# Turning activation tiles with VectorE blocks and ScalarE copies in place of TensorE transposes

## The chip, the cores and the metric

The kernel runs on one core of one Trainium2 chip. The metric is device time in microseconds, from the first to the last instruction of one execution, as the median over runs. TensorE (PE) does matrix products into PSUM, its weight loads (PEld) run beside them; VectorE (DVE) and ScalarE (ACT) work elementwise; GpSimd (POOL) does almost nothing here; SyncE (SP) issues the DMAs.

## The reference

One decoder layer, 256 tokens of 2048 channels, all float32: a SwiGLU FFN (5632 wide), a mixer with two branches, a second FFN. Each is normalised, modulated by a conditioning vector c through w_ada, and added to x. Cut to what matters:

```python
mod = (silu(c) @ w_ada + b_ada).reshape(B, 9, 1, D)

h = modulate(rms_norm(x, g_ffn1), mod[:, 0], mod[:, 1])
x = x + 0.5 * mod[:, 2] * swiglu(h, w_ffn1_gu, w_ffn1_down)    # (silu(g) * u) @ w_down

h = modulate(rms_norm(x, g_mix), mod[:, 3], mod[:, 4])
u_pool, q, k, v, ga, gb = split(h @ w_in)
y_pool = multiscale_pool(u_pool, pool_mix, pool_scale) @ w_pool_up
y_attn = swa_sink_attention(q, k, v, ...) @ w_attn_up
merged = sigmoid(ga) * y_pool + sigmoid(gb) * y_attn
x = x + mod[:, 5] * (merged @ w_o)

h = modulate(rms_norm(x, g_ffn2), mod[:, 6], mod[:, 7])
x = x + 0.5 * mod[:, 8] * swiglu(h, w_ffn2_gu, w_ffn2_down)
```

## The kernel before

**Sets.** Every large product is a `Set`: up to 1024 output columns, for both tiles of 128 tokens, over all rows of the weight. The stationary operand is a block of 128 channels by 128 tokens, so activations are kept with channels on the partitions; the weight rows move. Four PSUM banks hold a set's sums (two token tiles by two chunks of 512 columns); the other four banks, `bank()`, serve small work and then the next set. A ktile is 128 rows of a weight. `run` (line 205) goes over the ktiles: each load brings 1 MB, two ktiles at 1024 columns or four at 512, into a `raw` tile, of which there are six (`RAW`).

**Split products.** Each float32 product is three: hi*hi, lo*hi, hi*lo. `prep` (line 172) makes the halves of a weight ktile: ScalarE copies it rounded (`wh`, line 180), VectorE subtracts (`wl`, line 184). There are three buffers of each. `mm` (line 187) issues the products, lines 194, 196 and 198. Activations that come from a turned tile are split by `split_stat` just ahead of their product (lines 297 and 298: `sh` and `sl`, or `hh` and `hl`).

**Order.** The program says what is done in a dictionary of hooks after which ktile. A scheduler then draws up each engine's order at compile time: of what is ready, the instruction that stands first in the program goes first, so that an engine can do later work while it would wait. A tile's buffer is taken from the free ones when its first instruction can go.

**FFN.** `ffn` (line 400) takes the 5632 activation columns in pieces of 1024, the last of 512. For each piece a set makes the gate products, `silu_to` (line 386) brings them to SBUF as `sg`, another set makes the up products, and `times` (line 391) multiplies, on VectorE (line 395). The result has tokens on the partitions; the down product needs channels there. `store_T` (line 378) returns the pieces of that turn, and the next set runs them after its ktile 3. For each two blocks of 128 channels, `pair_T` (line 221) has TensorE transpose four 128x128 blocks into one PSUM bank (line 225), and ScalarE copies the bank to the tile `actT` (line 382; its name in the profile is `big`). The first FFN's first three pieces are finished together during the first norm, their parts waiting inside `actT` and in `sg`, and all three are turned in the set after them. After the last piece come two down sets of 44 ktiles.

**Mixer.** The merged rows come in two halves of 1024 columns. Each is finished by lines 736 and 737 on VectorE, and turned into `mT` (line 742) in the same way as above, by `tr` at ktile 3 of the next set: the next gate set for the first half, the output projection w_o for the second. The projection uses the second half from its ktile 8 on.

**Side work.** Sums over w_ada for later stages run beside the products: `ada_item` loads 1 MB into a `raw` tile and adds it up on VectorE (line 129). 0.82 such items go with each weight load in the first FFN, 0.56 in the mixer, 0.15 in the second FFN.

Of the kernel before, what the change touches and what calls it, by code (L numbers as in the profile page):

```python
# [15 lines left out]
P = 128  # L16
D = 2048
S = 256
T = S // P
# [7 lines left out]
EPS = 1e-6  # L27
NEG = -1e30
CW = 512
SW = 1024  # L30
NB = 32
TOE = 384
RAW = 6
T2 = 3
TAIL = 4
# [4 lines left out]
def trunk_layer(ctx, tc, x, c, w_ada, b_ada, g_ffn1, w_ffn1_gu, w_ffn1_down, g_mix, w_in,  # L40
                pool_mix, pool_scale, w_pool_up, q_gain, k_gain, sinks, rel_bias, w_attn_up,
                w_o, g_ffn2, w_ffn2_gu, w_ffn2_down, pool_w, onehot, out):
    nc = tc.nc
    pool = lambda name, bufs=1, **kw: ctx.enter_context(tc.tile_pool(name=name, bufs=bufs, **kw))
# [12 lines left out]

    # Eight PSUM banks in two groups of four: one holds the running set's accumulators, the
    # other serves everything small until the next set takes it.
    cur, rr = [0], [0]  # L60
# [7 lines left out]

# [1 line left out]
    ident = const.tile([P, P], F32, name="ident")  # L70
# [3 lines left out]
    ones = const.tile([P, P], F32R, name="ones")  # L74
# [8 lines left out]

# [1 line left out]
    # Each partition sums its 16 rows of w_ada; a matrix of ones then sums the partitions.  # L85
    ada_v = w_ada[0].rearrange("(k p) n -> p k n", p=P)
# [12 lines left out]
    def mod_col(j, b, c0):  # L99
        """Sums that lie alike on all partitions, to a column for each 128 channels."""  # L100
        k, n = c0 // P, b.shape[1] // P
        d = t_([P, n, P], "t2", T2)
        nc.vector.tensor_tensor(d, b.rearrange("p (a q) -> p a q", a=n),
                                ident.unsqueeze(1).to_broadcast([P, n, P]), ALU.mult)
        m = mcol[:, j, k:k + n]
        nc.vector.tensor_reduce(m, d, AX.X, ALU.add)
        i, o = j // 3, j % 3
        bc = bcol[:, (2 * i + o) * KD + k:(2 * i + o) * KD + k + n]
        if o == 0:
            nc.vector.tensor_tensor(m, m, bc, ALU.add)  # L110
        else:
            nc.vector.scalar_tensor_tensor(out=m, in0=m, scalar=1.0, in1=bc, op0=ALU.add, op1=ALU.add)
            nc.vector.tensor_tensor(m, m, gcol[:, i * KD + k:i * KD + k + n], ALU.mult)

    def ada_item(j, c0, i, a):
        """An eighth of the sum for SW columns of one of the nine vectors."""
        if i == 0:
            a.append(t_([P, SW], "acc", 2))
            if j % 3 == 2:
                nc.gpsimd.memset(a[0], 0.0)  # L120
                nc.sync.dma_start(a[0][0:1, :], b_ada[0:1, j * D + c0:j * D + c0 + SW])
        raw = t_([P, 2, SW], "raw", RAW)
        nc.sync.dma_start(raw, ada_v[:, 2 * i:2 * i + 2, j * D + c0:j * D + c0 + SW])
        for k in range(2):
            sc = cs[:, 2 * i + k:2 * i + k + 1]
            if i == k == 0 and j % 3 != 2:
                nc.vector.tensor_scalar_mul(a[0], raw[:, k, :], sc)
            else:
                nc.vector.scalar_tensor_tensor(out=a[0], in0=raw[:, k, :], scalar=sc, in1=a[0],  # L129
                                               op0=ALU.mult, op1=ALU.add)  # L130
        if i < 7:
            return
        for o in range(0, SW, CW):
            b = bank()
            acc_sum(b, a[0][:, o:o + CW])
            if j % 3 == 2:
                if j not in gates:
                    gates[j] = t_([P, D], "gate", 1)
                nc.scalar.activation(gates[j][:, c0 + o:c0 + o + CW], b, AF.Copy, scale=1.0 if j == 5 else 0.5)
            else:  # L140
                mod_col(j, b, c0 + o)
# [12 lines left out]

# [1 line left out]
    class Set:  # L156
# [64 lines left out]
    def pair_T(src, f0, dst_fn):  # L221
        b = bank()
        for f in range(2):
            for t in range(T):
                nc.tensor.transpose(b[:, (2 * f + t) * P:(2 * f + t + 1) * P], src(t, f0 + f), ident)  # L225
        dst_fn(f0, b)

# [1 line left out]
    # sums of squares over D / 2, a last column holding twice EPS: their sum is twice the variance  # L229
    ssq = const.tile([P, T, 5], F32, name="ssq")  # L230
# [8 lines left out]
    def rsqrt2(v2, s0, r0, a):  # L239
        """r0 * a = 1 / sqrt(v2 / 2), by a Newton step from the engine's root."""  # L240
        nc.scalar.activation(s0, v2, AF.Sqrt, scale=0.5)
        nc.vector.reciprocal(r0, s0)
        if v2.shape[1] == 1:
            nc.vector.scalar_tensor_tensor(out=a, in0=v2, scalar=r0, in1=r0, op0=ALU.mult, op1=ALU.mult)
        else:
            nc.vector.tensor_tensor(a, r0, r0, ALU.mult)
            nc.vector.tensor_tensor(a, a, v2, ALU.mult)
        nc.vector.tensor_scalar(a, a, -0.25, 1.5, ALU.mult, ALU.add)
# [41 lines left out]

# [1 line left out]
    def split_stat(src, kept=None):  # L292
        """Halves of src, two ktiles at a time; some stay for another set if there is room."""
        cache = {}
# [32 lines left out]

    # ---- the last products of a phase and the first of the next, one token tile after the other,
    # so that each tile's sums, norm and transposes run under the other's products ----
    def tail(s, c0, jgate, after):  # L330
        """The last TAIL ktiles of a set; yields after each token tile's products."""
        items = []
        for ka in range(s.nk - TAIL, s.nk, 2):
            raw = s.load(ka, 2)
# [43 lines left out]
    def store_T(src, f0, n, actT):  # L378
        """Transposes of act columns, to be called once the next set runs."""
        def dst(f, b):  # L380
            k = f0 // P + f
            nc.scalar.copy(actT[:, k:k + 2, :].rearrange("p a b -> p (a b)"), b)

        return [lambda f=f: pair_T(lambda t, f: src[:, t, f * P:(f + 1) * P], f, dst) for f in range(0, n // P, 2)]

# [10 lines left out]

    def hook(fs):
        return {3: lambda: [f() for f in fs]} if fs else None

    def ffn(w_gu, w_down, hh, hl, actT, f0, pend, sg, g, jgate, after):  # L400
        """From act column f0 on, g holding the gate products there; up to the last set's tail."""
        stat = lambda k: (hh[:, k, :], hl[:, k, :])
# [23 lines left out]

    # ---- first norm: its scale and shift come in column blocks, and with each block the
    # first sets of products go on; their sums wait in SBUF ----
    x_sb = const.tile([P, T, D], F32, name="x_sb")

    def ada_block(c0, w, shared):
        """The pieces of the first shift and scale at w columns. The rows of w_ada are summed on
        each partition, or, if shared, every other one goes through the tensor engine."""
        acc, banks = [], []
# [26 lines left out]
    nc.sync.dma_start(x_sb, x[0].rearrange("(t p) d -> p t d", p=P))  # L461
    # norm gains, pool scale and the biases of shifts and scales: a column for each 128 channels
    KG, KB = 3 * KD + PW // P, 6 * KD
# [68 lines left out]

# [1 line left out]
    WI = w_in[0]  # L534
    QO, KO, UO, GA, GB = PW, PW + NH * HD, 0, PW + NH * HD + 2 * NKV * HD, PW + NH * HD + 2 * NKV * HD + D

    # relative bias as a Toeplitz table in DRAM: column a holds distance a - 127
    rel = const.tile([NB + 1, NH], F32, name="rel")
# [63 lines left out]
    def qk_norm():  # L602
# [14 lines left out]
        for a in range(0, 8, 2):  # L617
            def dst(f0, b):
                nc.scalar.activation(qT[:, f0:f0 + 2, :].rearrange("p a b -> p (a b)"), b, AF.Copy, scale=gq[:, 0:1])
            pair_T(lambda t, f: q_sb[:, t, f * P:(f + 1) * P], a, dst)  # L620
        # keys and values in falling order of position
        b = bank()
# [47 lines left out]
    def heads_out(h0):  # L670
        l, kv = lg, h0 // 8
        pT = t_([P, 3, HB, P], "sg", 1)
        for i in range(HB):
# [3 lines left out]
            nc.scalar.copy(pT[:, :, i, :], b.rearrange("p (g q) -> p g q", g=3))  # L677
        # even heads fill the lower half of the partitions, odd heads the upper
        b1 = bank((P, 2, P))
# [7 lines left out]
        a = h0 // 2  # L687
# [35 lines left out]
    for half_ in range(2):  # L723
# [14 lines left out]

        def tr(sgb=sgb, half_=half_):
            def dst(f, b):  # L740
                k = half_ * 8 + f
                nc.scalar.copy(mT[:, k:k + 2, :].rearrange("p a b -> p (a b)"), b)
            for f in range(0, 8, 2):
                pair_T(lambda t, f: sgb[:, t, f * P:(f + 1) * P], f, dst)
        hk = {3: tr}
    residual(run(Set(w_o[0], KD, (0, SW), split_stat(mT)), hk), 0, 5, sumsq)
# [4 lines left out]

# [1 line left out]
    ov = out[0].rearrange("(t p) d -> p t d", p=P)  # L753
# [18 lines left out]
def _shape_constants():  # L772
    import numpy as np

    # pooling as a product over positions: mean over the window, less the token itself
    pw = np.zeros((4, P, TOE), np.float32)
    for g, w in enumerate(POOL_WINDOWS):
# [6 lines left out]
        pw[g, :, S:] = full[P:, P:]  # L784
    # bucket of each distance, one-hot; row NB marks what the window leaves out
    n = np.arange(TOE) - (P - 1)
# [33 lines left out]
```

## Time and profile before

| | |
|---|---|
| median of 3 runs | 2041.13 us (2040.59 to 2041.98) |
| the profiled execution (span) | 2041.3 us, 23823 instructions |
| TensorE busy | 2008.7 us, 98% |
| VectorE busy | 1472.2 us, 72% |
| ScalarE busy | 987.3 us, 48% |
| mean granted TensorE clock | 0.998 |
| HBM read | 520.00 MB, 256 GB/s over the span |

The profile is of one execution. A row of a group of instructions gives line, engine, operation, the tile written and the tile read, the shapes and the count; then the time the group was busy, not counting overlap with the instruction before it on its engine, and the mean duration of one in ns; then the engine's idle time just before these instructions and what ended it. In a timeline a row is the start, the length, the engine and the instructions merged in it. Matmuls overlap, so their durations add up to more than the time they occupy: the distance between starts shows that. Windows are counted from the start of the span.

### The profile page before, as it was taken

The numbers are of one execution on the slowest core, as the hardware profiler recorded it, in microseconds if no ns is written. First come the engines' busy times: TensorE is split into PE (matmuls) and PEld (weight loads), VectorE is DVE, ScalarE is ACT, GpSimd is POOL, SyncE is SP. The second block draws the span as 40 slices with busy tenths as digits, with TensorE's granted clock in tenths as the row PEclk, the third lists the DMA queues.
The fourth block names the chain that finished last, engine by engine and source line by source line (L and its number), as shares of the span: only waits on it lengthen the run. The fifth ranks groups of instructions, "written<-read, shape, count | busy, mean of one in ns | idle before, by whom it ended". The sixth has DMA issues, their size and how long they took to land. (4 is left out here: it accounts for less than half of the span.)

```text
span 2041.3 us, 23823 instructions
## 1 busy us (share of the span) xinstructions
PE 2008.7 (98%) x9053; PEld 1648.5 (81%) x9053; DVE 1472.2 (72%) x1698; ACT 987.3 (48%) x1324; POOL 7.3 (0%) x17
## 2 busy tenths in 40 slices
PE   6999999999999999999999999999999999999999
PEld 4788888888788887888788887788888888888887
DVE  5799878788899956777878788755555555566645
ACT  3554454444544546546554455654443444454443
POOL 0000000000000000000000000000000000000000
PEclk9999999999999999999999999999999999999999
DMA  9988758998898855776868887455655656666762
GB/s 337 356 316 301 279 198 305 334 338 313 318 350 334 333 195 183 252 278 229 293 237 288 292 283 270 165 209 207 243 206 206 228 204 214 219 223 231 233 193 69
DMA packets 157915, 523.69 MB, mean 257 GB/s; under 512 B 9353, under 2 KB 23394, under 8 KB 157544
## 3 DMA queue, kind: packets, MB, share of 16 engines
q1 hardware_dynamic: 157800, 522.16, 72.2%
q8 instruction: 71, 1.16, 0.2%
q14 instruction: 44, 0.36, 0.0%
HBM read 520.00 MB, written 2.12 MB: 256 GB/s over the span
## 5 line engine op out<-in xcount | busy, mean ns | idle before, releaser
L180 ACT CAST wh<-raw 128x1024 fp32r<-128x1024 f32 (+2 forms) x731 | 730.9, 1003 | 949.6 <-PE bank L196 874.2
L184 DVE TENSOR_TENSOR wl<-raw,wh 128x1024 fp32r<-128x1024 f32 (+2 forms) x746 | 842.0, 1136 | 452.2 <-ACT wh L180 447.2
L194 PE MATMUL bank<-wh,hh 128*128 128x512 f32 x2072 | 654.5, 390 | 6.7 <-ACT hh L278 5.7
L198 PE MATMUL bank<-wl,hh 128*128 128x512 f32 x2072 | 651.8, 389 | 0.8 <-DVE wl L184 0.5
L196 PE MATMUL bank<-wh,hl 128*128 128x512 f32 x2072 | 652.1, 389 | 0.0
L194 PEld LDWEIGHTS bank<-wh,hh 128*128 128x128 f32 x2072 | 387.1, 188 | 88.4 <-ACT hh L278 7.8
L198 PEld LDWEIGHTS bank<-wl,hh 128*128 128x128 f32 x2072 | 389.0, 188 | 83.4 <-DVE wl L184 3.9
L196 PEld LDWEIGHTS bank<-wh,hl 128*128 128x128 f32 x2072 | 388.7, 188 | 81.5 <-DVE hl L279 1.4
L129 DVE SCALAR_TENSOR_TENSOR acc<-raw,cs,acc 128x1024 f32<-128x1024 f32 x216 | 276.4, 1279 | 41.2 <-DMA raw<-in_w_ada_dram 39.4
L198 PE MATMUL bank<-wl,sh 128*128 128x512 f32 x692 | 216.9, 390 | 1.9 <-DVE wl L184 1.9
L196 PE MATMUL bank<-wh,sl 128*128 128x512 f32 x692 | 216.6, 390 | 0.3 <-DVE sl L298 0.3
L194 PE MATMUL bank<-wh,sh 128*128 128x512 f32 x692 | 216.7, 390 | 0.0
L198 PEld LDWEIGHTS bank<-wl,sh 128*128 128x128 f32 x692 | 129.7, 188 | 29.6 <-DVE wl L184 2.8
L194 PEld LDWEIGHTS bank<-wh,sh 128*128 128x128 f32 x692 | 129.7, 188 | 28.6 <-ACT wh L180 0.6
L196 PEld LDWEIGHTS bank<-wh,sl 128*128 128x128 f32 x692 | 129.8, 188 | 27.9 <-DVE sl L298 1.0
L452 DVE SCALAR_TENSOR_TENSOR acc<-raw,cs,acc 128x1024 f32<-128x1024 f32 (+1 forms) x59 | 68.1, 1154 | 7.0 <-DMA raw<-in_w_ada_dram 6.2
L298 DVE TENSOR_TENSOR sl<-big,sh 128x512 fp32r<-128x512 f32 x88 | 60.0, 683 | 4.2 <-ACT sh L297 4.2
L297 ACT CAST sh<-big 128x512 fp32r<-128x512 f32 x88 | 54.3, 621 | 8.1 <-DVE big L652 8.1
L522 DVE TENSOR_TENSOR big<-bank,big 128x512 f32<-128x512 f32 x60 | 38.1, 682 | 1.2 <-PE bank L198 0.8
L276 ACT ACTIVATE t<-bank,mcol 128x128 f32<-128x128 f32 x90 | 35.0, 463 | 7.8 <-PE bank L264 7.1
L236 ACT ACTIVATE junk<-x_sb 128x512 bf16<-128x512 f32 x24 | 15.1, 629 | 19.9 <-DVE x_sb L322 13.8
L448 PE MATMUL bank<-raw,cs 128*128 128x256 f32 x64 | 19.4, 458 | 3.3 <-DMA raw<-in_w_ada_dram 3.3
(156 smaller groups left out, 698.2 us busy)
## 6 DMA issues: line engine op xcount, KB each, us to landing
raw<-in_w_ffn_gu_dram SPq DMA_DIRECT2D x176, 1024.0 KB, 5.0
raw<-in_w_ada_dram SPq DMA_DIRECT2D x112, 1024.0 KB, 6.4
raw<-in_w_ffn_down_dram SPq DMA_DIRECT2D x88, 1024.0 KB, 5.8
raw<-in_w_in_dram SPq DMA_DIRECT2D x48, 1024.0 KB, 5.0
raw<-in_w_ada_dram SPq DMA_DIRECT2D x64, 512.0 KB, 7.5
raw<-in_w_o_dram SPq DMA_DIRECT2D x16, 1024.0 KB, 7.1
raw<-in_w_pool_up_dram SPq DMA_DIRECT2D x8, 1024.0 KB, 6.9
raw<-in_w_attn_up_dram SPq DMA_DIRECT2D x8, 1024.0 KB, 5.6
```

The lines of the kernel that those rows point to most:

```text
L129: nc.vector.scalar_tensor_tensor(out=a[0], in0=raw[:, k, :], scalar=sc, in1=a[0], op0=ALU.mult, op1=ALU.add)
L180: nc.scalar.copy(wh, raw_k)
L184: nc.vector.tensor_tensor(wl[:, e], raw_k[:, e], wh[:, e].bitcast(F32), ALU.subtract)
L194: nc.tensor.matmul(self.banks[t][i], hi[:, sl], wh[:, o], start=first, stop=False)
L196: nc.tensor.matmul(self.banks[t][i], lo[:, sl], wh[:, o], start=False, stop=False)
L198: nc.tensor.matmul(self.banks[t][i], hi[:, sl], wl[:, o], start=False, stop=last)
L276: nc.scalar.activation(h[:, f, :], src, AF.Identity, scale=g_, bias=b_)
L297: nc.scalar.copy(hi, src[:, k:k + n, :])
L298: nc.vector.tensor_tensor(lo, src[:, k:k + n, :], hi.bitcast(F32), ALU.subtract)
L448: nc.tensor.matmul(banks[j], sc.to_broadcast([P, P]), r[:, j, :], start=kk == 0, stop=False)
L452: nc.vector.scalar_tensor_tensor(out=acc[0], in0=r, scalar=sc, in1=acc[0], op0=ALU.mult, op1=ALU.add)
L522: nc.vector.tensor_tensor(a, b, a, ALU.add)
```

## The change

The turn of the FFN activations and of the merged rows no longer uses TensorE. VectorE transposes the tile in blocks of 32x32 elements, which stay in their quarter of the partitions: one instruction for each token tile, into a tile `z` that takes one of the six `raw` buffers. ScalarE then copies 32 partitions at a time from quarter i to quarter j, sixteen copies for a piece, each for all its channels and both token tiles, so that 32-token runs lie where `actT` or `mT` wants them. The PSUM banks and the evictions of the old way are gone. The eighteen instructions of a piece are spread by `hook` over the ktiles of the next set: at most `ks` hooks, beginning after ktile 1, so two after each ktile for one piece over 15 hooks, four for the three pieces together, and three for the second half of the merged rows, which has six hooks. The transposes of queries and attention weights stay on TensorE.

```diff
@@ def store_T(src, f0, n, actT):
-        """Transposes of act columns, to be called once the next set runs."""
-        def dst(f, b):
-            k = f0 // P + f
-            nc.scalar.copy(actT[:, k:k + 2, :].rearrange("p a b -> p (a b)"), b)
-
-        return [lambda f=f: pair_T(lambda t, f: src[:, t, f * P:(f + 1) * P], f, dst) for f in range(0, n // P, 2)]
+        z = []
+
+        def blocks(t):
+            if not z:
+                z.append(t_([P, T, n], "raw", RAW))
+            nc.vector.transpose(z[0][:, t, :], src[:, t, 0:n])
+
+        def move(i, j):
+            k, m = f0 // P, n // P
+            nc.scalar.copy(actT[32 * j:32 * j + 32, k:k + m, :].rearrange("p k (t i r) -> p k t i r", t=T, i=4)[:, :, :, i, :],
+                           z[0][32 * i:32 * i + 32].rearrange("p t (k j r) -> p k t j r", j=4, r=32)[:, :, :, j, :])
+
+        return [lambda t=t: blocks(t) for t in range(T)] + [lambda i=i, j=j: move(i, j) for i in range(4) for j in range(4)]
...
-    def hook(fs):
-        return {3: lambda: [f() for f in fs]} if fs else None
+    def hook(fs, other=None, ks=15):
+        hk, q = dict(other or {}), -(-len(fs) // ks)
+        for i in range(0, len(fs), q or 1):
+            k, o = 1 + i // q, hk.get(1 + i // q)
+            hk[k] = lambda o=o, p=fs[i:i + q]: [f() for f in ([o] if o else []) + p]
+        return hk
...
-        def tr(sgb=sgb, half_=half_):
-            def dst(f, b):
-                k = half_ * 8 + f
-                nc.scalar.copy(mT[:, k:k + 2, :].rearrange("p a b -> p (a b)"), b)
-            for f in range(0, 8, 2):
-                pair_T(lambda t, f: sgb[:, t, f * P:(f + 1) * P], f, dst)
-        hk = {3: tr}
+        hk = hook(store_T(sgb, half_ * SW, SW, mT), None, 15 if half_ == 0 else 6)
```

## The prediction

> **What bounds the kernel now.** I read the page's totals and slices first, then the waits, then the groups by line with shapes kept apart, and last the timeline around the transposes. Of the page, busy time by engine and the slices for TensorE, VectorE, ScalarE and the DMA engines:
>
> ```profile
> PE 2008.7 (98%) x9053; PEld 1648.5 (81%) x9053; DVE 1472.2 (72%) x1698; ACT 987.3 (48%) x1324; POOL 7.3 (0%) x17
> ...
> PE   6999999999999999999999999999999999999999
> DVE  5799878788899956777878788755555555566645
> ACT  3554454444544546546554455654443444454443
> ```
>
> TensorE is busy in all but the first slice; the other engines have room everywhere. So an instruction taken off TensorE shortens the run by what it occupies there, and work put on the others costs nothing until a split weight comes late. The waits say how far from late they are; the columns are total, times, longest:
>
> ```profile
> ACT wh L180 <- PE bank L196: 874.2, 588, 3.8
> ...
> SPq L169 <- DVE wl L184: 992.7, 243, 11.4
> ```
>
> ScalarE's split (wh) waits for TensorE to give a buffer back, never the other way in any amount, and the load queue waits for a free raw tile. Each stage runs ahead until its buffers are full.
>
> **What is removed.** TensorE loses 208 transposes: 88 in each FFN (44 ktiles, two token tiles) and 32 for the merged rows. The groups count 224, 16 of which turn queries and stay. Duration is the mean; the number before it is busy time not yet covered by another PE instruction:
>
> ```profile
> L225 PE MATMUL bank<-ident,sg 128*128 128x128 f32 x176 | 21.3, 272 | 0.0
> L225 PE MATMUL bank<-ident,big 128*128 128x128 f32 x48 | 5.8, 274 | 0.0
> ```
>
> What they occupy is read from the starts, as matmuls overlap. The timeline of PE at a block of 48 and at one of 16:
>
> ```profile
> 325.02 0.62 PE L198 MATMUL bank<-wl,hh 128*128 128x512 f32 x2
> 325.48 3.65 PE L225 MATMUL bank<-ident,big 128*128 128x128 f32 x32
> ...
> 330.64 0.71 PE L194 MATMUL bank<-wh,hh 128*128 128x512 f32 x2
> 331.19 0.63 PE L196 MATMUL bank<-wh,hl 128*128 128x512 f32 x2
> ...
> 418.04 0.62 PE L196 MATMUL bank<-wh,hl 128*128 128x512 f32 x2
> 418.50 0.62 PE L198 MATMUL bank<-wl,hh 128*128 128x512 f32 x2
> 418.95 1.91 PE L225 MATMUL bank<-ident,sg 128*128 128x128 f32 x16
> 420.62 0.72 PE L194 MATMUL bank<-wh,hh 128*128 128x512 f32 x2
> 421.17 0.62 PE L196 MATMUL bank<-wh,hl 128*128 128x512 f32 x2
> ```
>
> A pair of matmuls comes every 0.455 us (418.04 to 418.50), so a ktile at 1024 columns, six pairs, takes 2.72 us and one at 512 columns 1.36. From 418.50 to 421.17 there are two such steps and the block: 2.67 - 0.91 = 1.76 us for 16. In the same way, for the 48 (the view splits them by tile, 32 and 16), 331.19 - 325.02 - 0.91 = 5.26 us. There are eight blocks of 16 at a hook, two of 8 (half: 0.88 each), the one of 48, and the last sixteen at the output projection, taken at 1.8: 5.26 + 14.1 + 1.76 + 1.8 = 22.9 us. The page "TensorE: Matmul & The Clock Gate" of the Trainium skill (Part 4, PE-mode transpose) gives about 275 ns for such a transpose inside a kernel; the rows' 272 ns agree as a duration, but the starts show 0.11 us each, so taking 275 ns for each would estimate 57 us, which I don't expect.
>
> **What is added, and what covers it.** Fourteen turned tiles: 28 VectorE block transposes (24 of 128x1024, four of 128x512) and 224 ScalarE copies of 32 partitions (192 of 512 elements, 32 of 256); 52 ScalarE evictions go. No row shows either new form. The nearest, with line 382 and 742 as the evictions that go:
>
> ```profile
> L184 DVE TENSOR_TENSOR wl<-raw,wh 128x1024 fp32r<-128x1024 f32 x636 | 772.6, 1221 | 412.1 <-ACT wh L180 409.3 <-DMA acc<-in_b_ada_dram 1.5
> L180 ACT CAST wh<-raw 128x1024 fp32r<-128x1024 f32 x651 | 684.5, 1055 | 890.7 <-PE bank L196 840.1 <-DMA raw<-in_w_ffn_gu_dram 19.9 <-DVE wl L184 10.8
> L297 ACT CAST sh<-big 128x512 fp32r<-128x512 f32 x88 | 54.3, 621 | 8.1 <-DVE big L652 8.1
> L180 ACT CAST wh<-raw 128x512 fp32r<-128x512 f32 x64 | 39.9, 623 | 51.0 <-PE bank L196 26.7 <-DVE wl L184 22.1 <-DVE acc L129 2.1
> L382 ACT COPY big<-bank 128x512 f32<-128x512 f32 x44 | 22.4, 609 | 0.1
> L127 DVE TENSOR_SCALAR acc<-raw,cs 128x1024 f32<-128x1024 f32 x8 | 6.0, 749 | 1.6 <-DMA raw<-in_w_ada_dram 1.6
> L655 DVE TENSOR_REDUCE am<-big 128x4 f32<-128x1024 f32 x4 | 4.8, 1206 | 0.0
> L579 ACT COPY big<-bank 128x256 f32<-128x256 f32 x2 | 0.6, 370 | 0.0
> ```
>
> VectorE transpose of 1024: from 0.75 us (line 127) to 2.4 (two passes of line 655's 1.206); I take 1.2, as it has one source and no arithmetic. Twenty-eight of them add about 31 us to VectorE. The page "VectorE: DVE Perf Modes" of the Trainium skill (The three transpose paths) has 311 ns for 128x128 bf16 on VectorE, and its rules for kernel authors send a 128x128 transpose to TensorE; eight times that would be an estimate of 2.5 us for 1024 columns, and by it the time would be some 2042, where the third rival begins to decide. No run here shows it yet.
>
> ScalarE copy of 512 elements: the free size is that of line 297, the partitions fewer; between 0.37 (line 579) and 1.06 us (line 180, were the 32-element runs to halve the rate). I take 0.62 alone and 0.51 back to back (line 382's busy time over its count). That adds 192 x 0.62 + 32 x 0.37 - 52 x 0.51 = 104 us to ScalarE, 48% to 53%. It matters by stage:
>
> ```profile
> 325.00:370.00 45.00, 45.00 (x225) 38.06 (x224) 34.13 (x30) 25.90 (x35) 0.00 (x0) 1.00 0.85 310
> 547.00:570.00 23.00, 23.00 (x105) 18.63 (x104) 23.00 (x30) 14.09 (x21) 0.00 (x0) 1.00 0.88 327
> 1752.00:1798.00 46.00, 46.00 (x213) 38.34 (x212) 26.54 (x37) 25.88 (x41) 0.00 (x0) 1.00 0.64 209
> ```
>
> (Columns: window, length, busy PE, PEld, DVE, ACT, POOL, granted clock, DMA share, GB/s.)
> - Sets of 1024 columns, two moves a hook: ScalarE has 1.06 + 2 x 0.51 to 0.62, at most 2.3 us, of each 2.72. Hidden. Without that cover a set would lose 8 hooks x the excess.
> - The set at 325 us, 48 moves: 25.9 - 12 x 0.51 + 48 x 0.51 = 44 of 45 us, but its first parts are complete before it starts, so some moves go earlier. I take 0, bound 3.
> - VectorE at a set's start: two transposes, 2.4 us, now stand after wl(1) and before wl(2). At 1024 columns wl(2) is needed two ktiles, 5.4 us, in; 0.5 us for eight such starts together, bound 4.
> - Gate sets of 512 columns, one in each FFN: a ktile is 1.36 us, so the same 2.4 us meets less slack. VectorE's timeline there, and at the output projection:
>
> ```profile
> 498.54 2.47 DVE L395 TENSOR_TENSOR sg<-bank,sg 128x512 f32<-128x512 f32 x4
> 500.94 1.28 DVE L184 TENSOR_TENSOR wl<-raw,wh 128x512 fp32r<-128x512 f32 x2
> ...
> 1748.09 2.65 DVE L395 TENSOR_TENSOR sg<-bank,sg 128x512 f32<-128x512 f32 x4 [0.24 <-PE bank L198]
> 1750.65 1.50 DVE L184 TENSOR_TENSOR wl<-raw,wh 128x512 fp32r<-128x512 f32 x2
> ...
> 1208.52 1.28 DVE L737 TENSOR_TENSOR sg<-sg,big 128x512 f32<-128x512 f32 x2
> 1209.72 2.35 DVE L184 TENSOR_TENSOR wl<-raw,wh 128x1024 fp32r<-128x1024 f32 x2
> ```
>
> ```profile
> 504.46 1.91 PE L225 MATMUL bank<-ident,sg 128*128 128x128 f32 x16
> ...
> 1754.92 1.91 PE L225 MATMUL bank<-ident,sg 128*128 128x128 f32 x16
> ...
> 1210.43 0.93 PE L225 MATMUL bank<-ident,sg 128*128 128x128 f32 x7
> 1211.12 1.19 PE L198 MATMUL bank<-wl,sh 128*128 128x512 f32 x4
> ```
>
> The transposes at 504.46 follow ktile 3, so that set began four ktiles, 5.44 us, earlier, at 499.0, and needs wl(2) at 499.0 + 2.72 + 0.45 = 502.2; it came at 501.6. Pushed by 2.4 it is 1.8 us late. In the second FFN, by the same reckoning, the set began at 1749.5 and needs wl(2) at 1752.6; it came at 1751.3, so it is 1.1 us late. ScalarE adds: 0.62 + 2 x 0.51 = 1.64 us a ktile against 1.36, over eight hooks 2.2 us, about what three wh buffers hold. I take 2 us for each gate set, 4 in all; bounds 0 and 8.
> - Output projection: at 1211.12 four matmuls start just after wl ends (1209.72 + 1.22), and seven transposes stood in that gap; 0.7 us of their time remains as a wait. The turned tile then goes ahead of wl(2): 2 us late. Its sixteen moves, three a hook, must end before ktile 8 is split, about 22 us into the set; from 1213, 16 x 0.51 plus five wh and three halves make some 16 us, so they end in time. 2.7 us in all, bounds 0 and 8.
> - Raw tiles: the turned tile takes one of six, for up to eight ktiles, 22 us, and no DMA is added. The load queue is moved past it: five tiles in place of six. Five hold ten ktiles, 27 us; with modulation loads beside them (0.82 for each weight load) 15 us. The landing must stay under that:
>
> ```profile
> raw<-in_w_ffn_gu_dram SPq DMA_DIRECT2D x176, 1024.0 KB, 5.0
> raw<-in_w_ada_dram SPq DMA_DIRECT2D x112, 1024.0 KB, 6.4
> ```
>
> 5.0 and 6.4 us do, so 0; without that cover a set loses one tile's time, 5.44/1.82 = 3 us, at four sets of the first FFN.
>
> Sum against the profiled execution's span of 2041.3 us, 0.2 us over the median of 2041.13: 2041.3 - 22.9 + 0.5 + 4 + 2.7 = 2025.6. I say 2025.5.
>
> **The rivals.**
> 1. ScalarE's copies are slow and feed TensorE late. For: runs of 32 elements, and VectorE is full at 547 to 570 us, so nothing catches up there. Against: ScalarE's 48%. At 1.06 us a copy, a 512-column gate has 0.62 + 2.1 = 2.7 us a ktile against 1.36: 8 x 1.38 - 2.4 of lead = 8.6 us, twice; the 1024 sets lose 8 x 0.46 less a lead of about 5, nothing; the projection 5 more. 22 us: the gain is gone, 2041.
> 2. Every transpose frees its whole 0.272 us: 208 x 0.272 = 57 us, 1985. The duration in the group's row speaks for it, the starts at 418 us against. The page on TensorE named above gives this figure.
> 3. The other side: VectorE's transposes hold up wl(2) at every set. The pair is hidden at 1024 columns up to some 3 us, and a start is late by what exceeds that. There are twelve starts with a turned tile, so the loss equals the gain at 22.9/12 = 1.9 us each: it decides from about 2.5 us a transpose. At four passes of 1.2, 4.8 us, the pair takes 9.6 us, some 6 us late at each start: 2041 - 23 + 12 x 6 = 2090. Only the form that no row shows speaks for it; line 655's rate against. The rule for kernel authors named above, TensorE for a 128x128 transpose, would be borne out by it.
>
> **How the numbers follow.** My case 0.77, rival 1 0.08, rival 2 0.02, rival 3 0.13. The measurement tells 0.2% (4 us) from no change, so faster is under 2037: 0.79; same (rival 1) 0.08; slower (rival 3) 0.13. My case alone is 2016 to 2036: 2018.4 without any late term, and 2 us below it because every engine's order is drawn up anew and other waits may shrink; 2018.4 + 8 + 8 at the bounds of the gates and the projection. With rival 1's 2041 the range 2016 to 2042 holds over 0.8.
>
> **What would show it.** Line 225 falls to 16 transposes; PE's instructions by 208, its busy time by 23 to 25 us. A new VectorE group at 1.2 us x24 and ScalarE copies near 0.6 us x192. ScalarE near 1090 us, VectorE near 1500. PE waits on wl or wh at the 512-column gates, near 490 and 1740 us, and at the projection near 1200; none at 1024 columns. I am wrong if the transposes take over 2 us, if copies take 1 us, or if PE waits on raw tiles' DMA.

## The result, and the profile after

The kernel became slower: 2103.61 us median (2101.87 to 2107.01) against 2041.56 for the kernel before on the same chip, a ratio of 1.0304 [1.0290, 1.0319]. The prediction of 2025.5 (2016 to 2042) was wrong, in sign too. The totals of the profile's page after:

```profile
span 2100.1 us, 23599 instructions
...
PE 2014.3 (96%) x8845; PEld 1638.8 (78%) x8845; DVE 1503.0 (72%) x1726; ACT 1089.7 (52%) x1496; POOL 7.3 (0%) x17
```

TensorE has 208 instructions fewer and is nevertheless busy for 5.6 us more. Both totals forecast for the other engines came out (1503.0 for 1500, 1089.7 for 1090). So did the durations of one instruction, in the groups by line with shapes kept apart:

```profile
L390 ACT COPY big<-raw 32x512 f32<-32x512 f32 x192 | 118.6, 618 | 44.2 <-DVE raw L386 41.1 <-DVE sg L541 0.6
...
L386 DVE STREAM_TRANSPOSE raw<-sg 128x1024 f32<-128x1024 f32 x20 | 23.6, 1217 | 0.0
...
L390 ACT COPY big<-raw 32x256 f32<-32x256 f32 x32 | 12.9, 402 | 0.4
...
L225 PE MATMUL bank<-ident,big 128*128 128x128 f32 x16 | 2.1, 276 | 0.0
```

(The other four transposes of 1024 columns read `big`, at 1.223 us each; the four of 512 took 0.692.)

The new thing is the idle time in the first row: ScalarE sat 41.1 us in front of its moves, waiting for VectorE's transposes. TensorE's waits before and after (total, times, longest):

```profile
PE bank L194 <- ACT wh L180: 1.0, 2, 0.5
```

```profile
PE bank L194 <- ACT wh L180: 49.2, 20, 8.9
...
PE bank L196 <- DVE sl L298: 4.2, 2, 2.4
```

TensorE now waits 49 us for weight splits that ScalarE used to have ready. How this comes about is seen at any of four like places in the second FFN; here the timelines of ScalarE, VectorE and TensorE at one of them (start, length, instructions, idle time before them and its releaser):

```profile
1427.17 1.05 ACT L180 CAST wh<-raw 128x1024 fp32r<-128x1024 f32 x1 [1.67 <-PE bank L196]
1429.89 1.05 ACT L180 CAST wh<-raw 128x1024 fp32r<-128x1024 f32 x1 [1.67 <-PE bank L196]
1436.90 3.14 ACT L390 COPY big<-raw 32x512 f32<-32x512 f32 x5 [5.96 <-DVE raw L386]
1440.06 1.99 ACT L180 CAST wh<-raw 128x1024 fp32r<-128x1024 f32 x2
...
1432.12 2.47 DVE L404 TENSOR_TENSOR sg<-bank,sg 128x512 f32<-128x512 f32 x4
1434.51 2.36 DVE L386 STREAM_TRANSPOSE raw<-sg 128x1024 f32<-128x1024 f32 x2
...
1437.85 0.61 PE L198 MATMUL bank<-wl,hh 128*128 128x512 f32 x2
1441.16 0.82 PE L194 MATMUL bank<-wh,hh 128*128 128x512 f32 x2 [2.70 <-ACT wh L180]
1441.77 1.06 PE L196 MATMUL bank<-wh,hl 128*128 128x512 f32 x2
1442.63 1.06 PE L194 MATMUL bank<-wh,hh 128*128 128x512 f32 x2
1443.48 1.06 PE L198 MATMUL bank<-wl,hh 128*128 128x512 f32 x2
1444.33 0.98 PE L196 MATMUL bank<-wh,hl 128*128 128x512 f32 x2
1445.15 0.62 PE L198 MATMUL bank<-wl,hh 128*128 128x512 f32 x2
```

A split comes every 2.72 us, so the next was due at 1432.61. In ScalarE's order five moves stand in front of it. They need the transposes, and those need the products of line 404, which need the end of the up set: the moves stand at the head of the queue for 5.96 us, then run for 3.14, and the split starts at 1440.06, 7.45 us late. The buffers cover 4.75 us of that; TensorE stands for 2.70. Then it goes on at half pace: pairs every 0.85 us in place of 0.455. The windows around it (length, busy PE, PEld, DVE, ACT, POOL, granted clock, DMA share, GB/s) and the mean clock of the run:

```profile
1429.50:1441.20 11.70, 9.00 (x41) 7.14 (x39) 5.96 (x8) 5.28 (x8) 0.00 (x0) 1.00 0.37 138
1441.20:1445.20 4.00, 4.00 (x11) 3.17 (x12) 2.44 (x3) 3.75 (x5) 0.00 (x0) 0.57 0.17 42
1445.20:1450.00 4.80, 4.80 (x23) 3.98 (x22) 3.16 (x3) 4.19 (x6) 0.00 (x0) 1.00 0.78 259
```

```profile
core 0: 2100.1 us, clock 0.985
```

In four of these microseconds the clock is 0.57, that is 3.4 us at a half; 1.7 us are lost, more than half as much as the wait. Over the run (1 - 0.985) x 2100.1 = 31 us are lost to the clock, against (1 - 0.998) x 2041.3 = 4 before. The account: 2041.3 - 22.9 (transposes) + 48 (more waiting for wh) + 27 (clock) = 2093.4; of the other 7 us to 2100.1, 4.2 are the wait for sl shown above, and the rest is shorter waits.

By place, as the time by which consecutive 512-column matmuls are more than 0.227 us apart, summed over the trace (22.9 us before, only by chance the same number as that of the transposes, and some 4 of them near the places below; 103.5 after), against what the prediction allowed:

| place | predicted | measured |
|---|---|---|
| first FFN, set with 48 moves (320 to 377) | 0 | 5.8 |
| eight sets of 1024 columns: first FFN at 410 (7.2), mixer at 1104 (7.9), second FFN (four times 4.55), the two down sets at 561 (10.4) and 1854 (5.5) | 0.5 | 49 |
| gate sets of 512 columns (506 and 1804) | 4 | 14.6 |
| end of the first FFN (682 to 707) | not priced | 6.3 |
| output projection (1244 to 1257) | 2.7 | 10.7 |

### The profile page after: what moved, and what is told of

Same layout as the page of the kernel before. It is cut to its first block, busy times and chain, and to the rows that moved or that the text cites. A ratio compares the mean times of both kernels' runs of the same rounds, so it can differ in the third digit from the quotient of the medians.

```text
span 2100.1 us, 23599 instructions
## 1 busy us (share of the span) xinstructions
PE 2014.3 (96%) x8845; PEld 1638.8 (78%) x8845; DVE 1503.0 (72%) x1726; ACT 1089.7 (52%) x1496; POOL 7.3 (0%) x17
## 4 chain that ended last, share of the span: by engine, by line
PE 85%; DVE 6%; ACT 5%; issue 2%; DMA 2%; SPq 0%; DVEq 0%; ACTq 0%
PE bank L194 27%; PE bank L196 27%; PE bank L198 27%; ACT big L390 3%; DVE wl L184 1%; ACT wh L180 1%; DMA raw<-in_w_ada_dram 1%; DVE raw L386 1%; DVE sg L404 1%; PE bank L264 0%; DVE acc L129 0%; DMA x_sb<-in_x_dram 0%; PE bank L462 0%; DVE t L321 0%; PE bank L97 0%
## 5 line engine op out<-in xcount | busy, mean ns | idle before, releaser
L194 PE MATMUL bank<-wh,hh 128*128 128x512 f32 x2072 | 661.3, 393 | 33.9 <-ACT wh L180 28.3
L194 PEld LDWEIGHTS bank<-wh,sh 128*128 128x128 f32 x692 | 131.3, 190 | 51.0 <-ACT wh L180 22.9
L390 ACT COPY big<-raw 32x512 f32<-32x512 f32 (+1 forms) x224 | 131.4, 587 | 44.6 <-DVE raw L386 41.1
L94 ACT CAST t<-acc 128x512 fp32r<-128x512 f32 x28 | 17.0, 619 | 26.3 <-DVE acc L129 23.1
```

What stands on the lines that cost most here:

```text
L194: nc.tensor.matmul(self.banks[t][i], hi[:, sl], wh[:, o], start=first, stop=False)
L390: nc.scalar.copy(actT[32 * j:32 * j + 32, k:k + m, :].rearrange("p k (t i r) -> p k t i r", t=T, i=4)[:, :, :, i, :], z[0][32 * i:32 * i + ...
```

## The experiments

The theory (A in the expectations): the loss is one of order. ScalarE works through a list drawn up at compile time; moves stand in it ahead of splits that are ready, and wait there. Its rivals: the moves' own time on ScalarE is too much (B); VectorE's transposes hold up the residues `wl` (C); the lost raw tile delays the loads (D). Ratios are to the kernel before, run on the same chip.

| run | median us | ratio [95%] | mean clock |
|---|---|---|---|
| e1, moves behind their ktile's split | 2061.54 | 1.0106 [1.0089, 1.0123] | 0.993 |
| e2, moves that wait for nothing | 2080.48 | 1.0194 [1.0179, 1.0209] | 0.990 |
| e3, before + VectorE transposes | 2069.62 | 1.0144 [1.0129, 1.0159] | 0.996 |
| e4, before + TensorE transposes twice | 2067.80 | 1.0135 [1.0116, 1.0154] | 0.998 |
| e5, e1's order for transposes too | 2069.35 | 1.0138 [1.0123, 1.0153] | 0.990 |
| e6, e5 and the other side work ordered | 2064.32 | 1.0114 [1.0097, 1.0131] | 0.992 |
| e7, before with e6's rules | 2044.43 | 1.0018 [1.0008, 1.0027] | 0.999 |
| e8, ordered moves in one burst | 2102.35 | 1.0301 [1.0286, 1.0317] | 0.986 |
| e9, new path at five pieces only | 2029.46 | 0.9942 [0.9929, 0.9954] | 0.999 |
| e10, e6 with the moves spread thinner | 2045.30 | 1.0020 [1.0010, 1.0029] | 0.995 |
| e11, before with five raw tiles | 2043.62 | 1.0017 [1.0008, 1.0027] | 0.998 |

**e1: the order of the moves alone.** Each move stands behind the split of its hook's ktile in ScalarE's list (`issue_after`), from ktile 4 on where one piece is turned.

```diff
-            nc.scalar.copy(wh, raw_k)
+            last_wh[0] = nc.scalar.copy(wh, raw_k)
...
-            nc.scalar.copy(actT[32 * j:32 * j + 32, k:k + m, :]...
+            with tc.issue_after(last_wh[0].ins):
+                nc.scalar.copy(actT[32 * j:32 * j + 32, k:k + m, :]...
...
+        if len(fs) == 18:
+            n = 4 if ks == 6 else 2
+            hk[1] = lambda p=fs[:2]: [f() for f in p]
+            for i in range(2, 18, n):
+                hk[4 + (i - 2) // n] = lambda p=fs[i:i + n]: [f() for f in p]
+            return hk
```

> The changed kernel with all its instructions; only ScalarE's order is altered: each piece's moves stand behind the weight split (wh) of the ktile whose hook they belong to, from ktile 4 on (the three pieces together keep their hooks). Theory A, a queue blocked at its head (moves that wait for VectorE's transposes stand in ScalarE's order ahead of ready weight splits, in bursts, and TensorE runs dry): about 2021 us, between 2016 and 2028, PE waits on wh under 10 us. Theory B, too much ScalarE work: unchanged, near 2100. Theory C, VectorE's transposes delay wl: still over 2080. Theory D, the raw tile that is taken: over 2080.

Measured 2061.54: 42 of the 62 us are gone, 40 short of the forecast. ScalarE in a set of 1024 columns, and TensorE's waits:

```profile
1424.55 1.05 ACT L182 CAST wh<-raw 128x1024 fp32r<-128x1024 f32 x1 [0.39 <-PE bank L198]
1425.63 1.25 ACT L393 COPY big<-raw 32x512 f32<-32x512 f32 x2
1427.27 1.05 ACT L182 CAST wh<-raw 128x1024 fp32r<-128x1024 f32 x1 [0.39 <-PE bank L198]
1428.35 1.25 ACT L393 COPY big<-raw 32x512 f32<-32x512 f32 x2
```

```profile
PE bank L200 <- DVE wl L186: 15.0, 10, 5.8
PE bank L196 <- ACT wh L182: 7.9, 13, 1.7
```

This is what the prediction had in mind: 1.05 + 1.25 us of every 2.72, and 0.39 us to spare. The four places of the second FFN lose nothing now. What remains lies in the first set, the 512-column gates, the down sets and the projection. Of TensorE's waits for wh, wl and sl beyond those before, about half are for wl (15.0 us, before 2.5).

**e8: the same order rule, one burst.** As e1, but all sixteen moves at ktile 4.

```diff
-            for i in range(2, 18, n):
-                hk[4 + (i - 2) // n] = lambda p=fs[i:i + n]: [f() for f in p]
+            hk[4] = lambda p=fs[2:]: [f() for f in p]
```

> As e1_order, but all sixteen moves of a piece stand at one hook, behind the wh of ktile 4, so that none waits long for a transpose. Theory A, in its part that a burst of 16 x 0.62 us ahead of wh outlasts the lead of the three wh buffers: 2 to 4 us lost at each 1024-column start and about 7 at each 512-column gate, 2090 to 2105 us in all. If only the wait for the transposes cost time: 2061.

Measured 2102.35, as expected: the loss is back. ScalarE's and TensorE's timelines:

```profile
1432.40 1.05 ACT L182 CAST wh<-raw 128x1024 fp32r<-128x1024 f32 x1 [1.67 <-PE bank L198]
1433.36 10.05 ACT L393 COPY big<-raw 32x512 f32<-32x512 f32 x16
1443.43 2.94 ACT L182 CAST wh<-raw 128x1024 fp32r<-128x1024 f32 x3
```

```profile
1440.36 0.61 PE L200 MATMUL bank<-wl,hh 128*128 128x512 f32 x2
1444.53 1.22 PE L196 MATMUL bank<-wh,hh 128*128 128x512 f32 x2 [3.55 <-ACT wh L182]
1445.55 1.05 PE L198 MATMUL bank<-wh,hl 128*128 128x512 f32 x2
1446.40 1.05 PE L200 MATMUL bank<-wl,hh 128*128 128x512 f32 x2
```

No move waits here for a transpose; the burst alone makes the split due at 1435.12 late by 8.31 us, and TensorE stands for 3.55. Again 4.76 us are covered, as above (7.45 - 2.70). So it does not matter whether ScalarE idles or copies in front of the split; more than 4.75 us of either and TensorE stands, at 1024 columns. Half clock follows again.

**e2: moves that wait for nothing.** They read rows of x, which are always there, and the transposes stay.

```diff
-                           z[0][32 * i:32 * i + 32]...
+                           x_sb[32 * i:32 * i + 32, :, 0:n]...
```

> The changed kernel with its transposes and all 224 copies of the same sizes, but the copies read rows of x, which lie ready long before, so the activations of the down products and of w_o are wrong. No copy waits for a transpose; the turned tile is given back at once. Theory A: 2017 to 2028 us. Theory B: near 2100, as ScalarE's 131 us of copies are all there. Theory C: over 2080. Theory D, the raw tile: also 2017 to 2028.

Missed: 2080.48, not 2017 to 2028; it lies at the edge of what stood for rival C (over 2080). The waits of the moves for transposes are gone from ScalarE's list, but with nothing to wait for, the moves were drawn forward. ScalarE at the start of the second FFN:

```profile
1359.65 1.88 ACT L390 COPY big<-x_sb 32x512 f32<-32x512 f32 x3
1361.55 1.05 ACT L180 CAST wh<-raw 128x1024 fp32r<-128x1024 f32 x1
1362.63 1.88 ACT L390 COPY big<-x_sb 32x512 f32<-32x512 f32 x3
1364.53 1.05 ACT L180 CAST wh<-raw 128x1024 fp32r<-128x1024 f32 x1
```

Three a split need 1.05 + 1.88 = 2.93 us of 2.72: ScalarE became the bound there. The edit changed the rate as well as the wait, so it separates less than was hoped; it shows that a move's wait is not needed for the loss. Nor does it clear rival C, as TensorE's waits for wl grew from 2.5 us before to 20.0, more than the 11.3 for wh:

```profile
PE bank L198 <- DVE wl L184: 20.0, 12, 5.8
```

**e3: VectorE's half alone.** The kernel before, with 28 transposes that nobody reads put at the same hooks.

```diff
-        return [lambda f=f: pair_T(...) for f in range(0, n // P, 2)]
+        return [lambda t=t: blocks(t) for t in range(T)] + [lambda f=f: pair_T(...) for f in range(0, n // P, 2)]
```

> The kernel before, with the 28 VectorE transposes added into a raw tile that nobody reads; TensorE's transposes stay. Theories A and B: 2041 to 2047 us. Theory C: at least 2080. Theory D, with the raw tile given back at once: 2041 to 2047.

Missed by both sides: 2069.62, between the two. The added instructions take some 32 us of an engine that is 72% busy and cost 29. ScalarE's waits for TensorE's bank ahead of line 382's evictions grew to 30.2 us (before, line 382 idled 0.1 us in all), and TensorE's waits for wh and wl with them, from 1.0 and 2.5:

```profile
PE bank L194 <- ACT wh L180: 13.6, 10, 2.2
...
PE bank L198 <- DVE wl L184: 6.5, 2, 4.8
...
ACT big L382 <- PE bank L225: 30.2, 7, 8.0
```

So work added to VectorE alone moves ScalarE's order too, since one scheduler draws up both. How much of the 29 us is that and how much VectorE's time at the first FFN, where it is full, this run does not say. Its trace gives the places: at the sets of the first four pieces of the second FFN nothing is lost, but from 535 to 578 us, at the first down set, matmuls come some 10 us late, with the wait of 4.8 us for wl above among them. That is as much as the changed kernel loses there, without a single move.

**e4: the price of TensorE's transposes.** The kernel before, each of the 208 issued twice.

```diff
-                nc.tensor.transpose(b[...], src(t, f0 + f), ident)
+                for _ in range(reps):
+                    nc.tensor.transpose(b[...], src(t, f0 + f), ident)
```

> The kernel before, with each of the 208 TensorE transposes of store_T and tr issued twice. By the starts in the timeline (0.11 us each) 2041.5 + 22.9 = 2064 us; by the duration of a row (0.272 us each) 2098; if they fill time in which TensorE would wait anyway, 2041.

Measured 2067.80, 27.3 us over before by the medians and 24.7 by the spans (2066.0) for 208: 0.12 to 0.13 each, not 0.27. What leaves TensorE is worth what the starts said, within 5 us, and the second rival of the prediction is out.

**e5 and e6: more order.** e5 holds the transposes behind the residue (wl) of ktiles 3 and 4 and the moves from ktile 6; e6 also orders the activation splits (the last two edits below) and, in the same way, the sums over w_ada.

```diff
+            with tc.issue_after(last_wl[0].ins):
                 nc.vector.transpose(z[0][:, t, :], src[:, t, 0:n])
...
+            with tc.issue_after(last_wh[0].ins):
                 nc.scalar.copy(hi, src[:, k:k + n, :])
+            with tc.issue_after(last_wl[0].ins):
                 nc.vector.tensor_tensor(lo, src[:, k:k + n, :], hi.bitcast(F32), ALU.subtract)
```

> As e1_order, and VectorE's transposes too stand behind the wl of the ktile whose hook they belong to (hooks 3 and 4, moves from ktile 6; at w_o hooks 1 and 2, moves from ktile 4). Theory A extended (VectorE's queue is blocked at its head in the same way: transposes and the work hoisted beside them stand ahead of wl): about 2050 us, with the waits on wl at the 512-column gates and at w_o mostly gone and those at the first FFN's down set left. Theory B (what e1 still loses is work, not order): 2061.

> As e5_order_both, and the splits of activations (hi behind wh, lo behind wl) and the sums over w_ada (behind wl) are kept from running ahead of the weight splits as well. Theory A extended: 2020 to 2030 us, the gain of 22.9 nearly whole. Theory B: 2050 or more, because the first FFN's VectorE has no room for the transposes.

Both missed: 2069.35 and 2064.32, no better than e1. These rules gave no more; the first set grew worse, as its transposes, now behind wl, came later and its 48 moves ran inside the set, four a ktile. ScalarE there in e6:

```profile
327.38 2.50 ACT L397 COPY big<-raw 32x512 f32<-32x512 f32 x4
329.91 1.05 ACT L183 CAST wh<-raw 128x1024 fp32r<-128x1024 f32 x1
330.99 2.50 ACT L397 COPY big<-raw 32x512 f32<-32x512 f32 x4
333.51 1.05 ACT L183 CAST wh<-raw 128x1024 fp32r<-128x1024 f32 x1
```

A ktile takes 3.6 us (329.91 to 333.51) in place of 2.72.

**e7: the rules without the change.** The kernel before, with e6's rules for splits and sums.

> The kernel before with e6's order rules for activation splits and w_ada sums, and nothing else. It had little to lose to order, so both theories: 2037 to 2043 us; the difference from e6 is then what the change itself is worth under one rule of order.

Measured 2044.43, at most 5.5 us over before by the interval: the rules cost little. e6 is 20 us above it, so with the order given by hand the change was still a loss.

**e10: e6 with the moves spread thinner.** The 48 go over the gate and the up set, two a ktile; a 512-column gate gets one a ktile, and the up set the rest.

```diff
+                    if len(pend) == 54:
+                        p = pend[:36] + pend[36:38]
+                        late, pend = pend[38:], None
...
+                    elif len(pend) == 18 and fw < SW:
+                        hk = {3 + t: pend[t] for t in range(2)} | {6 + i: pend[2 + i] for i in range(8)}
+                        late = pend[10:]
...
-                    g = run(Set(w_gu, KD, (f0, fw), stat), hook(pend))
-                    pend = []
+                    g = run(Set(w_gu, KD, (f0, fw), stat), hk)
+                    pend = late
```

> The whole change in the order of the run before last of the ordered kind (splits and sums held too), with the moves spread thinner: the first set's 48 over the gate and the up set at two a ktile, the 512-column gates at one move a ktile and the rest in the up set. Theory (what was left at 2064 is rate: more moves a ktile than ScalarE has room for): the first set's 16 us fall to about 3 and the two 512-column gates' 10 to 4, so about 2045. Rival (what was left is not rate but the late start of the chain VectorE block, move, activation split): the losses at the first set stay and the time stays at 2060 to 2066.

Measured 2045.30, as the theory had it: rate is worth 19 us (by the ratios too, as e6 and e10 ran on different chips). The windows 320 to 376 of e6 and of e10:

```profile
320.00:376.00 56.00, 47.23 (x177) 35.72 (x176) 38.64 (x33) 47.78 (x68) 0.00 (x0) 0.91 0.68 249
```

```profile
320.00:376.00 56.00, 53.87 (x232) 43.05 (x232) 49.09 (x44) 49.11 (x68) 0.00 (x0) 1.00 0.83 308
```

The same count of ScalarE's instructions (68) with 55 matmuls more in the same time, at full clock. With this the whole change is within 0.3% of the kernel before. It still loses some 21 us in late places beyond before's: the first FFN's 512-column gate and down set (3.9 and 6.6), its end (6.1), the first set (about 4) and the projection (5.4), together 26 with what before loses there.

**e11: five raw tiles.**

```diff
-RAW = 6
+RAW = 5
```

> The kernel before with five raw tiles in place of six, which is what the turned tile leaves to the load queue while it lives. Theory (order, not tiles): 2040 to 2044, no weight tile lands late. Rival (the lost raw tile delays loads): 3 us at each set of the first FFN, 2050 or more, with waits of ScalarE on raw's DMA.

Measured 2043.62, +0.17%, with no wait of 3 us at every set. The lost tile is not the cause.

**e9: the new path only where it is covered.** The kernel before, with e5's order rule, for the first four pieces of the second FFN and the first half of the merged rows; TensorE turns the rest.

```diff
-            pend = store_T(sg, f0, fw, actT)
+            pend = (turn if jgate == 8 and f0 < 4 * SW else store_T)(sg, f0, fw, actT)
...
-        hk = {3: tr}
+        hk = turn(sgb, 0, SW, mT) if half_ == 0 else {3: tr}
```

> The kernel before, with the new path (VectorE blocks behind the weight residue of their ktile, ScalarE moves two a hook behind the weight split of theirs) only where the ordered runs showed no loss: the four full pieces of the second FFN, whose sets have 1024 columns, and the merged rows' first half. TensorE keeps its transposes elsewhere. Theory (the change is sound, its losses are of order and of local rate): five blocks of 16 leave TensorE, 5 x 1.76 = 8.8 us, and nothing comes late: 2031 to 2034. Rival (a move or a VectorE block costs TensorE time wherever it stands, as the 20 us left between the two fully ordered kernels could be read): five pieces of fourteen carry 5/14 x 43 = 15 us of cost against the 8.8: 2045 to 2049.

Measured 2029.46, 0.9942 [0.9929, 0.9954]: faster than the kernel before by its interval, and so than the changed one. Its groups and a window in the second FFN:

```profile
L401 ACT COPY big<-raw 32x512 f32<-32x512 f32 x80 | 49.5, 619 | 2.6 <-DVE raw L396 1.3
...
L227 PE MATMUL bank<-ident,sg 128*128 128x128 f32 x96 | 11.8, 272 | 0.0
```

```profile
1405.00:1500.00 95.00, 95.00 (x421) 78.67 (x420) 55.77 (x50) 53.37 (x63) 0.00 (x0) 1.00 0.66 230
```

Eighty moves waited 1.3 us in all for transposes, and TensorE was busy for all of the window at full clock. The 11 us of the medians (13.2 by the spans) are the 8.8 of five blocks and some waits elsewhere that became shorter (the sum of late matmuls fell from 22.9 to 18.7 us).

## Why the prediction was wrong

- **What is removed: right.** 22.9 us; e4 measured 25 to 27 for as many again; e9, with eighty fewer, is 11 us faster (8.8 forecast, the rest shorter waits).
- **Durations and totals: right.** 1.217 us a transpose for 1.2, 0.618 and 0.402 a move for 0.62 and 0.37. **The price back to back: wrong.** The 0.51 us came from the evictions; sixteen moves in a row took 10.05 us (e8), 0.63 each.
- **"Hidden" at 1024 columns: the step that failed.** It compared ScalarE's 2.3 us with the 2.72 of a ktile as if the two moves of a hook would come one pair a ktile. Nothing in the profile said so: a hook only says where an instruction stands in the program, and the list drawn up from that had five to sixteen moves in a row ahead of a split. The step asked what a move costs, never what is queued behind a move that waits. e1 shows the step true under its unspoken condition (0.39 us to spare, no loss), e8 shows the loss return with that condition alone taken away. The line "Without that cover a set would lose 8 hooks x the excess" was the wrong form too: the loss is lateness less 4.75 us, plus the half clock behind it.
- **Set of 48 moves, "I take 0": failed.** At 0.63 us a move its sum gives 25.9 - 6.1 + 30.2 = 50 us of ScalarE in 45, not 44. The cover was said to be that some moves go earlier. In the changed kernel they began at 316.1 us, and 5.8 us were lost, over the bound of 3; in e6 they began at 321.4, and some 16 were lost. In both a ktile with four moves took 3.6 us.
- **Gate sets 4 us and projection 2.7, bounds 8 each: too small,** 14.6 and 10.7, both beyond their bounds. The pushed wl was priced; the burst of moves ahead of wh was not. The worst of the 1024-column places looks like the same case: at the first down set sixteen moves of 0.4 us stand in one burst of 6.6 us. But e3 loses as much there without moves, so this place's cause is not shown.
- **Raw tile 0: right** to about 3 us (e11).
- **The range:** its upper end has an error too. 2018.4 + 8 + 8 is 2034.4, not 2036, and the bounds of 3 and 4 us stated for two other terms are not in it.
- **What a wait costs beyond itself: not priced.** Some 27 us of half clock, against a profile before whose clock was 0.998 and showed it only at its ends.
- **Rival 3 gave 2090, near the result, for a reason that is out.** It needed 2.5 us a transpose and more, and they took 1.2. At 1.2 they are not free either: in e3 the kernel before with them added is 29 us slower, where the prediction had 7.2 for all late terms together. **Rival 1** needed copies of 1.06 us. Neither asked for the order. The prediction also missed what TensorE's transposes did besides costing time: while ScalarE ran twelve evictions in a row at 326 us before (5.96 us), TensorE was itself turning for 5.26 us, and so did not run out of splits (its waits for wh are 1.0 us in all). With the turn on other engines, TensorE consumes splits during the moves. ScalarE's row of before:

```profile
326.18 5.96 ACT L382 COPY big<-bank 128x512 f32<-128x512 f32 x12
```

Open: why the scheduler put the moves where it did; how much of the loss in the first FFN is VectorE's transposes by themselves; and the last 21 us of e10, of which the places are known but no run took one away by itself.

## What to carry to other kernels

Work moved to an idle engine is hidden only if its place in that engine's order is known: find the instruction that the bottleneck waits for next, ask what will stand in front of it, for how long it can be late (here 4.75 us, three buffers), and what the front one is itself waiting for. Issue such work in pieces smaller than the slack of one step, behind that step's critical instruction, and move only the stages that have slack (e9). Add to each wait of TensorE the time that it takes to come back to full clock.

## What was not expected of the hardware

The granted clock falls to a half after a wait in the middle of the kernel, in stretches of 3.4 us. The trace shows it behind the wait of 2.70 us above; where waits follow each other it is longer (1245 to 1260 us, at the projection: a mean clock of 0.66 in 15 us, so 10.2 us). The length of a wait alone does not decide it: in e10 one of 3.29 us passed without it, with pairs 0.45 us apart at once:

```profile
1222.43 0.73 PE L199 MATMUL bank<-wh,sl 128*128 128x512 f32 x2 [3.29 <-DVE sl L303]
1223.00 0.62 PE L201 MATMUL bank<-wl,sh 128*128 128x512 f32 x2
1223.46 0.40 PE L197 MATMUL bank<-wh,sh 128*128 128x512 f32 x1
```

Where the wait falls matters as well. In every trace the starts of the half-clock stretches lie whole multiples of 3.413 us apart (in the changed kernel, for instance, the four at 1441.68, 1533.84, 1626.00 and 1718.16, 27 such lengths from one to the next), so each trace can be cut into windows of that length at them. The wait of 2.70 us above lies inside one window (1438.27 to 1441.68); that of e10 is parted by a boundary, at 1220.69, into 1.55 and 1.74 us. Between the first 60 us and the last 7, the thirteen traces have 44 windows at full clock in which TensorE idled for more than 1.87 us, and half clock followed all 44; it followed none with less than 1.4 us, and 13 of the 45 in between.

The page "TensorE: Matmul & The Clock Gate" of the Trainium skill (Part 1) has the half rate and windows of about 3.4 us that run freely, with an idle window leading to half clock. The trace agrees with the half, with the 3.4 us and with windows that run on regardless of the waits; but the window need not be idle throughout: here 1.9 us of its 3.41 were enough.
